# A hybrid SSD, GLA and cross-attention layer on one core: products without priority, a padded row for the convolution, one table at first

## The chip, the core and the metric

The program runs on one core of one Trainium2 chip. Its engines are TensorE (PE in the profile; PEld is its weight load), VectorE (DVE), ScalarE (ACT), GpSimd (POOL) and SyncE (SP), which only issues transfers here. Each engine works its own queue in order and waits on semaphores of the others. The metric is the device time of one execution in microseconds (us).

## The reference

One inference step of one layer, for a prompt of 256 tokens and for 8 samples of 4 tokens each (288 columns together), D_MODEL 2048, everything in float32.

```
xn = rmsnorm(x)
z, xbc, dt, q, k, v, r, g_lr, gate_a, gate_b = split(xn @ w_in)
xbc = silu(causal_conv4(xbc, conv_state))       # 3072 channels, 3 earlier rows per sequence
branch_a = gated_norm(ssd_scan(xbc, dt), z) @ w_ssd_out      # 4 groups of 8 heads
branch_b = gated_norm(gla_scan(q, k, v, g_lr), r) @ w_gla_out   # 4 heads, state 256 x 512 each
h = x + (sigmoid(gate_a)*branch_a + sigmoid(gate_b)*branch_b) @ w_mix_out
h = h + cross_attend(rmsnorm(h), mem_k, mem_v)      # prompt memory is projected here, sample memory is an input
h = h + (silu(g) * a) @ w_down,  a, g = conv3(rmsnorm(h) @ w_up)
```

It returns the normed outputs, the new states of both scans and both convolutions, and the memory keys and values of the prompt.

## The kernel before

Activations lie with channels on the 128 partitions and the 288 tokens along the free axis, columns 0 to 255 for the prompt and 256 to 287 for the samples. Every weight is read once, by SP, in tiles `raw` of 4 x 128 rows by 256 columns (L108). Two halves of such a tile are split into two float32r tiles: `whi` by ACT (L101) and `wlo` by DVE (L103), five buffers each. A projection of 256 output channels (`proj_w`) makes, for one split, 12 products of 288 columns on PE: hi times hi and hi times lo (L133, L134), lo times hi (L137). Its two accumulators lie in two PSUM banks; two pairs of banks alternate. When the last split is through, `cons(j, a)` is called for each of the two output tiles and reads its bank.

The program has these stages: the memory projections with the norms of the memory and of x (from L377, where the statistics use Ln and Exp on ACT at L384, L385, L396, L397, and in `dt_prep`); then eight units, four SSD groups and four GLA heads; the merge; cross-attention; the ConvFFN.

In the eight units, two generators are woven: the projections of unit n + 1, with the output projection of unit n - 1 in their midst, are the main one, and the scan of unit n is the other. `weave` takes `n_bg` steps of the scan per `n_main` steps of the projections; the numbers are N_MAIN and N_BG. A `yield` ends a step. What is written in this order is then ordered per engine by a scheduler that takes the earliest written instruction that it holds ready, with its own estimate of times; an instruction may so pass others. `tc.high_priority(2000)` counts instructions as if they were written 2000 places earlier.

The SSD projections end in `conv_silu` (24 tiles: per group four of x, and for groups 0 and 2 two each of B and C): ACT writes the last tap with the bias from the bank into `out` (L582) and copies what else is wanted out of the bank (L583 to L585); DVE adds the other three taps, for the prompt from the bank (L592), for the samples from a small tile `sp` (L595) whose first three columns POOL has copied from the state (L587); ACT makes the tanh (L597), DVE the product (L598).

In `gla_scan` the samples' states (512 KB each, eight per head) are loaded by POOL's queue into tiles `sin`. Their products with the queries go to one bank `osa` in two groups of four states:

```
        for q in range(2):
            with tc.high_priority(2000):
                for k in (1, 0):
                    for j in (3, 2, 1, 0):
                        ...
                        MM(osa[...], qdm[:, k, b, :], sins[b][:, k, :], start=False, ...)
            yield
            for b in range(4 * q, 4 * q + 4):
                ...  # two products L1101, update of sin on DVE L1102, store by SP L1105, load of state b + 4
```

A tile `sin` of the second four takes the place of an earlier tile, so its load waits for that one's store to land. In `ssd_scan` the states are loaded in the same way (L682), transposed on PE (L833) and updated (L852).

Of the kernel before, what the change touches and what calls it, by code (L numbers as in the profile page):

```python
# [8 lines left out]
F32 = mybir.dt.float32  # L9
F32R = mybir.dt.float32r  # L10
I32 = mybir.dt.int32
ACT = mybir.ActivationFunctionType
ALU = mybir.AluOpType
# [3 lines left out]
P = 128  # L17
D = 2048
KT = D // P
SEQ = 256  # L20
NB = 8
NL = 4
NS = NB * NL
T = SEQ + NS
# [10 lines left out]
STOP = object()  # L35
N_MAIN = [64, 64, 48, 64, 64, 64, 64, 48]
N_BG = [58] * 4 + [42] * 4
# [3 lines left out]
def hybrid_step(ctx: ExitStack, tc: tile.TileContext, I: dict, O: list):  # L41
    nc = tc.nc
    (y_p, y_s, o_pconv, o_pssd, o_pgla, o_pffn, o_pmk, o_pmv, o_sconv, o_sssd, o_sgla, o_sffn) = O
    V, S, G = nc.vector, nc.scalar, nc.gpsimd
    MM, TR = nc.tensor.matmul, nc.tensor.transpose
# [30 lines left out]
    V.memset(epsc[:, 1:2], 4.0 * EPS)  # L76
    S.copy(epsc[:, 2:3], epsc[:, 0:1])
# [6 lines left out]
    vcol = const.tile([P, 116], F32, name="vcol")  # L84
    scw = const.tile([P, 96], F32, name="scw")
# [7 lines left out]
    def vec(name):  # L93
        o, n = vofs[name]
        return vcol[:, o:o + n]
# [133 lines left out]
    dtbd = p1.tile([P, 32 + 8], F32, name="dtbd")[:, 0:32]  # L229
# [5 lines left out]
    scst = p1.tile([P, 24, 24], F32, name="scst")  # L235
# [6 lines left out]
    for z in (cdm, att, ats, atsl.bitcast(F32), qdm, lr3.bitcast(F32), gw3.bitcast(F32), dtbd):  # L242
        G.memset(z, 0.0)
# [8 lines left out]
    with pool("p0") as p0:  # L252
# [170 lines left out]
        def x_prep():  # L423
# [15 lines left out]
            for q in range(2):  # L439
                a = mm_tile()  # L440
                for i in range(3):
                    TR(a[:, i * 96:(i + 1) * 96], srow[:, 3 * q + i, :], ident[0:96, 0:96])
                V.tensor_copy(scst[:, q * 12:(q + 1) * 12, :].rearrange("p t c -> p (t c)"), a[:, 0:288])
                yield
# [118 lines left out]

    def th_tile():
        return pa.tile([P, T], F32, tag="th", bufs=2, name="th")
# [13 lines left out]
    def conv_silu(ct, a, out, cache):  # L579
        cb_o = vofs["ssd_conv_b"][0]  # L580
        sp = pa.tile([P, NB, 8], F32, tag="sp", bufs=3, name="sp")
        S.activation(out, a, ACT.Identity, scale=scw[:, 72 + ct:73 + ct], bias=vcol[:, cb_o + ct:cb_o + ct + 1])  # L582
        S.copy(sp[:, :, 3:7], a[:, SEQ:T].rearrange("p (b l) -> p b l", l=NL))  # L583
        S.copy(cache[:, 0:3], a[:, SEQ - 3:SEQ])
        S.copy(cache[:, 3:27].rearrange("p (b k) -> p b k", k=3),  # L585
               a[:, SEQ:T].rearrange("p (b l) -> p b l", l=NL)[:, :, 1:NL])
        G.tensor_copy(sp[:, :, 0:3], scst[:, ct, :].rearrange("p (b k) -> p b k", k=3))  # L587
        outs = out[:, SEQ:T].rearrange("p (b l) -> p b l", l=NL)
        for k in range(3):
            s = 3 - k  # L590
            w = scw[:, 24 * k + ct:24 * k + ct + 1]
            V.scalar_tensor_tensor(out[:, s:SEQ], a[:, 0:SEQ - s], w, out[:, s:SEQ], ALU.mult, ALU.add)  # L592
        for k in range(3):
            w = scw[:, 24 * k + ct:24 * k + ct + 1]
            V.scalar_tensor_tensor(outs, sp[:, :, k:k + 4], w, outs, ALU.mult, ALU.add)  # L595
        th = th_tile()
        S.activation(th, out, ACT.Tanh)  # L597
        V.scalar_tensor_tensor(out, th, 1.0, out, ALU.add, ALU.mult)  # L598
# [61 lines left out]
    def ssd_scan(g, xsT, sz):  # L660
# [221 lines left out]
        yield  # L882
        yield from finish(sz, acc, vec("ssd_norm")[:, 4 * g:4 * g + 4], True)
# [98 lines left out]
    def gla_scan(h, eb, qe, ke, kd, kde, vT, sr):  # L982
# [104 lines left out]
        for q in range(2):  # L1087
            with tc.high_priority(2000):
                for k in (1, 0):
                    for j in (3, 2, 1, 0):  # L1090
                        b = 4 * q + j
                        MM(osa[NS * j:NS * j + NS, :], qdm[:, k, b, :], sins[b][:, k, :], start=False,
                           stop=(q == 1 and k == 0))
# [573 lines left out]
```

## Time and profile before

| | |
|---|---|
| median of 3 runs | 2626.22 us (2623.78 to 2627.47) |
| the profiled execution | 2624.57 us |
| its span, first to last instruction | 2622.9 us |
| PE busy | 2574.6 us, 98% |
| DVE busy | 1718.3 us, 66% |
| ACT busy | 1375.6 us, 52% |
| POOL busy | 315.1 us, 12% |
| moved from and to memory | 513.55 MB, 196 GB/s |

Busy is the time in which an engine has an instruction in work. Matmuls are pipelined, so a busy PE need not be at its peak. Idle time is put down to the semaphore that ended it. POOL's times are rough.

### The profile page before, as it was taken

The page shows a single profiled execution, that of the slowest core. Times are in us where ns is not written, and L with a number is a line of the kernel's source. Part 1 is how long each engine was busy: PE and PEld are TensorE (multiplying, and loading weights), DVE is VectorE, ACT ScalarE, POOL GpSimd, SP SyncE. Part 2 cuts the span into 40 slices and gives each one's busy share as a digit, 9 for nine tenths or more (in the row PEclk, how much of TensorE's full clock was granted, in tenths as well). Part 3 has the DMA queues.
Part 4 walks back from the last instruction along what each step waited for, and adds up shares of the span by engine and source line. Part 5 has one row for each costly group of instructions (what it writes and reads, how often), then busy time and mean ns, then how long its engine had stood idle before and what let it go on. Part 6 is the DMA issues. An engine that isn't in the chain of part 4 may idle for free. (4 is left out here: it accounts for less than half of the span.)

```text
span 2622.9 us, 50482 instructions
## 1 busy us (share of the span) xinstructions
PE 2574.6 (98%) x19119; PEld 2471.1 (94%) x19119; DVE 1718.3 (66%) x3680; ACT 1375.6 (52%) x2796; POOL 315.1 (12%) x443
## 2 busy tenths in 40 slices
PE   9999999999998999999999999999999999999998
PEld 7889999999997989898999988999999999999998
DVE  5656767686766656667656555567777677675765
ACT  7656456655453545354455544455545454454545
POOL 3002101010000000000000122202202011110200
PEclk9999999999999999999999999999999999999999
DMA  7676666566667565667766778655555555555553
GB/s 259 212 223 190 191 191 214 164 200 190 176 199 244 179 213 182 217 205 228 209 196 224 237 270 273 239 165 161 171 172 166 169 168 169 163 166 172 166 170 127
DMA packets 434768, 513.55 MB, mean 196 GB/s; under 512 B 23208, under 2 KB 384984, under 8 KB 434204
## 3 DMA queue, kind: packets, MB, share of 16 engines
q1 hardware_dynamic: 407532, 420.80, 52.0%
q0 software_dynamic: 26960, 89.52, 10.2%
q8 instruction: 150, 2.46, 0.4%
q14 instruction: 94, 0.77, 0.1%
q10 hardware_dynamic: 32, 0.01, 0.0%
HBM read 464.74 MB, written 45.48 MB: 195 GB/s over the span
## 5 line engine op out<-in xcount | busy, mean ns | idle before, releaser
L103 DVE TENSOR_TENSOR wlo<-raw,whi 128x512 fp32r<-128x512 f32 x1464 | 989.6, 689 | 711.0 <-ACT whi L101 695.6
L101 ACT CAST whi<-raw 128x512 fp32r<-128x512 f32 x1464 | 896.7, 618 | 1024.5 <-PE acc L134 816.0
L133 PE MATMUL acc<-xn,whi 128*128 128x288 f32 (+1 forms) x1936 | 553.9, 301 | 0.0
L134 PE MATMUL acc<-xn,whi 128*128 128x288 f32 (+1 forms) x1936 | 543.1, 296 | 0.0
L137 PE MATMUL acc<-xn,wlo 128*128 128x288 f32 (+1 forms) x1936 | 413.5, 295 | 0.3 <-DVE wlo L103 0.3
L133 PE MATMUL acc<-hf,whi 128*128 128x288 f32 x1408 | 396.5, 296 | 0.0
L134 PE MATMUL acc<-hf,whi 128*128 128x288 f32 x1408 | 393.9, 295 | 0.0
L134 PEld LDWEIGHTS acc<-xn,whi 128*128 128x128 f32 (+1 forms) x1936 | 365.4, 189 | 10.6 <-issue 8.3
L133 PEld LDWEIGHTS acc<-xn,whi 128*128 128x128 f32 (+1 forms) x1936 | 365.0, 189 | 5.8 <-issue 5.0
L137 PEld LDWEIGHTS acc<-xn,wlo 128*128 128x128 f32 (+1 forms) x1936 | 311.6, 188 | 0.9 <-DVE wlo L103 0.6
L137 PE MATMUL acc<-hf,wlo 128*128 128x288 f32 x1408 | 302.7, 297 | 0.0
L134 PEld LDWEIGHTS acc<-hf,whi 128*128 128x128 f32 x1408 | 265.5, 189 | 0.1
L133 PEld LDWEIGHTS acc<-hf,whi 128*128 128x128 f32 x1408 | 265.1, 188 | 0.1
L137 PEld LDWEIGHTS acc<-hf,wlo 128*128 128x128 f32 x1408 | 225.8, 188 | 0.0
L134 PE MATMUL acc<-pr,whi 128*128 128x288 f32 x704 | 196.9, 296 | 0.0
L133 PE MATMUL acc<-pr,whi 128*128 128x288 f32 x704 | 196.0, 294 | 0.0
L133 PE MATMUL acc<-un,whi 128*128 128x288 f32 x512 | 147.5, 304 | 3.8 <-DVE xsT L592 3.8
L137 PE MATMUL acc<-pr,wlo 128*128 128x288 f32 x704 | 148.0, 291 | 0.0
L1499 POOL COPY fsp<-fst 128x16 f32<-128x16 f32 x88 | 106.0, 1229 | 334.8 <-ACT fcg L1505 87.8
L134 PE MATMUL acc<-un,whi 128*128 128x288 f32 x512 | 143.4, 296 | 0.5 <-DVE un L171 0.5
L134 PEld LDWEIGHTS acc<-pr,whi 128*128 128x128 f32 x704 | 132.6, 188 | 0.0
L133 PEld LDWEIGHTS acc<-pr,whi 128*128 128x128 f32 x704 | 132.3, 188 | 0.0
(525 smaller groups left out, 4261.3 us busy)
## 6 DMA issues: line engine op xcount, KB each, us to landing
raw<-in_w_in_dram SPq DMA_DIRECT2D x240, 512.0 KB
raw<-in_w_up_dram SPq DMA_DIRECT2D x176, 512.0 KB
raw<-in_w_down_dram SPq DMA_DIRECT2D x88, 512.0 KB
raw<-in_w_ck_dram SPq DMA_DIRECT2D x32, 512.0 KB
raw<-in_w_cv_dram SPq DMA_DIRECT2D x32, 512.0 KB
raw<-in_w_ssd_out_dram SPq DMA_DIRECT2D x32, 512.0 KB
sin<-in_state_gla_dram POOLq DMA_DIRECT2D x32, 512.0 KB, 5.5
out_dram<-sin SPq DMA_DIRECT2D x32, 512.0 KB
```

What stands on the lines that cost most here:

```text
L101: S.copy(hi, raw)
L103: V.tensor_tensor(lo, raw, hi, ALU.subtract)
L133: MM(a, hi[:, k, cs], xh, start=(k0 + s0 + k == 0), stop=False)
L134: MM(a, hi[:, k, cs], xl, start=False, stop=False)
L137: MM(a, lo[:, k, cs], xh, start=False, stop=(k0 + s0 + k == nk - 1))
L1499: G.tensor_copy(sp[:, :, 0:2], st.rearrange("p (b k) -> p b k", k=2))
```

## The change

Five edits. The products of the sample states are written without `high_priority`. `conv_silu` works on one padded row per tile: eight stretches of 3 old and 4 new columns for the samples, then 3 zeros and the 256 columns of the prompt, 315 in all. ACT copies the bank into it (two copies), then all taps run over 312 columns of it; the tanh overwrites it, and two products write `out`. POOL copies the old rows into it and, from it, what the cache keeps. The padded row and the accumulator take tiles `th`, of which there are now three, shared with the tiles of the gates and scans as before. ACT loads one table that holds Ln and Exp at the start. `ssd_scan` has one more step ahead of the norm's sum, and N_BG grows by one for the SSD groups. `scst` gets room for three zero columns per tile, and is cleared.

```diff
-N_BG = [58] * 4 + [42] * 4
+N_BG = [59] * 4 + [42] * 4
...
+    S.preload_act_table_set(LNEXP)      # LNEXP = "natural_log_exp_and_others"
     S.copy(epsc[:, 2:3], epsc[:, 0:1])
...
-    scst = p1.tile([P, 24, 24], F32, name="scst")
+    scst = p1.tile([P, 24, 3 * NB + 3], F32, name="scst")
...
+    def cv_tile(name):
+        return pa.tile([P, 7 * NB + 3 + SEQ], F32, tag="th", bufs=3, name=name)
+
     def th_tile():
-        return pa.tile([P, T], F32, tag="th", bufs=2, name="th")
+        return cv_tile("th")[:, 0:T]
...
     def conv_silu(ct, a, out, cache):
...
-        S.activation(out, a, ACT.Identity, scale=scw[:, 72 + ct:73 + ct], bias=vcol[:, cb_o + ct:cb_o + ct + 1])
-        S.copy(sp[:, :, 3:7], a[:, SEQ:T].rearrange("p (b l) -> p b l", l=NL))
-        S.copy(cache[:, 0:3], a[:, SEQ - 3:SEQ])
-        S.copy(cache[:, 3:27]..., a[:, SEQ:T]...[:, :, 1:NL])
-        G.tensor_copy(sp[:, :, 0:3], scst[:, ct, :].rearrange("p (b k) -> p b k", k=3))
+        C = 7 * NB
+        cv, acc = cv_tile("cv"), cv_tile("cva")[:, 0:C + SEQ]
+        G.tensor_copy(by7(cv, 0, 3, NB + 1), scst[:, ct, :].rearrange("p (b k) -> p b k", k=3))
+        S.copy(cv[:, C + 3:], a[:, 0:SEQ])
+        S.copy(by7(cv, 3, NL, NB), a[:, SEQ:T].rearrange("p (b l) -> p b l", l=NL))
+        S.activation(acc, cv[:, 3:C + SEQ + 3], ACT.Identity, scale=..., bias=...)
+        G.tensor_copy(cache[:, 0:3], cv[:, C + SEQ:])
+        G.tensor_copy(cache[:, 3:27].rearrange("p (b k) -> p b k", k=3), by7(cv, 4, 3, NB))
         for k in range(3):
-            V.scalar_tensor_tensor(out[:, s:SEQ], a[:, 0:SEQ - s], w, out[:, s:SEQ], ALU.mult, ALU.add)
-        for k in range(3):
-            V.scalar_tensor_tensor(outs, sp[:, :, k:k + 4], w, outs, ALU.mult, ALU.add)
-        th = th_tile()
-        S.activation(th, out, ACT.Tanh)
-        V.scalar_tensor_tensor(out, th, 1.0, out, ALU.add, ALU.mult)
+            V.scalar_tensor_tensor(acc, cv[:, k:k + C + SEQ], scw[...], acc, ALU.mult, ALU.add)
+        th = cv[:, 0:C + SEQ]
+        S.activation(th, acc, ACT.Tanh)
+        V.scalar_tensor_tensor(out[:, 0:SEQ], th[:, C:], 1.0, acc[:, C:], ALU.add, ALU.mult)
+        V.scalar_tensor_tensor(out[:, SEQ:T]..., by7(th, 0, NL, NB), 1.0, by7(acc, 0, NL, NB), ALU.add, ALU.mult)
...
         yield
+        yield
         yield from finish(sz, acc, vec("ssd_norm")[:, 4 * g:4 * g + 4], True)
...
-            with tc.high_priority(2000):
-                for k in (1, 0):
+            for k in (1, 0):
```

In the orders below a line of the changed kernel is 2 to 8 higher than the same line before. First PE, around the second four states of the first GLA head, before: the products `la<-sin` stand in the midst of one split's weight products (`acc<-xn`), behind six of the update products `mm<-vst,kb` (six others stand ahead of these rows).

```order
L137 MATMUL acc<-xn_131,wlo 128x288 x2
L133 MATMUL acc<-xn_131,whi 128x288
L134 MATMUL acc<-xn_131,whi 128x288
L133 MATMUL acc<-xn_131,whi 128x288
L1092 MATMUL la<-sin,qdm 32x512 x8
L134 MATMUL acc<-xn_131,whi 128x288
L137 MATMUL acc<-xn_131,wlo 128x288 x2
L1101 MATMUL mm<-vst,kb 128x512
```

The same engine and place now, 54 rows further on (the products are L1099 here; two update products and 63 weight products have come ahead of them):

```order
L135 MATMUL acc<-xn_134,whi 128x288
L136 MATMUL acc<-xn_134,whi 128x288
L135 MATMUL acc<-xn_134,whi 128x288
L136 MATMUL acc<-xn_134,whi 128x288
L139 MATMUL acc<-xn_134,wlo 128x288 x2
L1099 MATMUL la<-sin,qdm 32x512 x8
L135 MATMUL acc<-xn_134,whi 128x288
```

The second four states now follow all eight update products of the first four; the first four keep their place.

Next ACT, the first two tiles of the convolution, before: `whi` is the weight cast, `acc` the bank that PE has filled, `th` the tanh.

```order
L582 ACTIVATE xsT<-acc,vcol,scw 128x288
L583 COPY sp<-acc 128x8x4
L584 COPY cache<-acc 128x3
L585 COPY cache<-acc 128x24
L101 CAST whi<-raw 128x512
L582 ACTIVATE xsT<-acc,vcol,scw 128x288
L583 COPY sp<-acc 128x8x4
L584 COPY cache<-acc 128x3
L585 COPY cache<-acc 128x24
L101 CAST whi<-raw 128x512
L597 ACTIVATE th<-xsT 128x288
```

And now, where `cv` is the padded row and `cva` the accumulator:

```order
L593 COPY cv<-acc 128x256
L594 COPY cv<-acc 128x8x4
L595 ACTIVATE cva<-cv,vcol,scw 128x312
L593 COPY cv<-acc 128x256
L594 COPY cv<-acc 128x8x4
L103 CAST whi<-raw 128x512 x2
L602 ACT_TABLE_LOAD
L602 ACTIVATE cv<-cva 128x312
L103 CAST whi<-raw 128x512 x2
L595 ACTIVATE cva<-cv,vcol,scw 128x312
L103 CAST whi<-raw 128x512 x2
L602 ACTIVATE cv<-cva 128x312
```

Both banks are read by the first five rows; the second tile's Identity and both tanhs stand between weight casts, and each waits for POOL and DVE.

Last POOL, around the last convolution tiles of the SSD groups and the third scan's states, before: `sp<-scst` is the copy of the old rows, `ab` the decays, `sin` the states of the third and fourth scan.

```order
L668 DMA ab<-acum_d 128x2x256
L587 COPY sp<-scst 128x8x3
L668 DMA ab<-acum_d 128x2x256
L587 COPY sp<-scst 128x8x3
L668 DMA ab<-acum_d 128x2x256
L587 COPY sp<-scst 128x8x3
L682 DMA sin<-in_state_ssd_dram 128x4x128 x16
```

And now:

```order
L592 COPY cv<-scst 128x9x3
L675 DMA ab<-acum_d 128x2x256
L597 COPY cache<-cv 128x3
L598 COPY cache<-cv 128x24
L592 COPY cv<-scst 128x9x3
L597 COPY cache<-cv 128x3
L598 COPY cache<-cv 128x24
L592 COPY cv<-scst 128x9x3
L597 COPY cache<-cv 128x3
L598 COPY cache<-cv 128x24
L689 DMA sin<-in_state_ssd_dram 128x4x128 x16
```

The copy of the old rows needed no result of the convolution's product; the cache copies do, and the state loads now stand behind the last of them.

## Rows read from the trace of the kernel before

**Rows 1.** The page, part 1: busy time, share of the span, instructions.

```profile
PE 2574.6 (98%) x19119; PEld 2471.1 (94%) x19119; DVE 1718.3 (66%) x3680; ACT 1375.6 (52%) x2796; POOL 315.1 (12%) x443
```

**Rows 2.** Waits of PE: who ended them; total us, times, longest us.

```profile
PE la L1092 <- DMA sin<-in_state_gla_dram: 23.6, 4, 7.8
PE acc L133 <- DVE xsT L592: 3.8, 3, 1.6
PE acc L319 <- ACT whi L101: 3.2, 3, 1.7
PE mm L890 <- DVE sqa L881: 1.7, 1, 1.7
```

**Rows 3.** PE's timeline at state products: start us, us, instruction, count, [idle before].

```profile
787.63 1.92 PE L1092 MATMUL la<-sin,qdm 128*32 128x512 f32 x16
...
817.31 3.64 PE L1092 MATMUL la<-sin,qdm 128*32 128x512 f32 x16 [7.76 <-DMA sin<-in_state_gla_dram]
...
946.84 3.64 PE L1092 MATMUL la<-sin,qdm 128*32 128x512 f32 x16 [6.49 <-DMA sin<-in_state_gla_dram]
...
1077.88 2.79 PE L1092 MATMUL la<-sin,qdm 128*32 128x512 f32 x12 [6.20 <-DMA sin<-in_state_gla_dram]
...
1194.39 3.35 PE L1092 MATMUL la<-sin,qdm 128*32 128x512 f32 x16 [3.13 <-DMA sin<-in_state_gla_dram]
```

**Rows 4.** Windows: length, busy (count) of PE, PEld, DVE, ACT, POOL; clock; DMA.

```profile
817.31:822.70 5.39, 5.39 (x23) 2.32 (x24) 0.26 (x1) 1.13 (x2) 0.00 (x0) 0.50 0.00 0
946.84:952.40 5.56, 5.56 (x24) 2.59 (x25) 0.21 (x1) 1.20 (x2) 0.00 (x0) 0.50 0.00 1
1077.88:1082.11 4.23, 4.23 (x19) 1.26 (x20) 0.00 (x0) 0.52 (x2) 0.00 (x0) 0.50 0.04 16
1194.75:1198.16 3.41, 3.41 (x18) 0.93 (x11) 0.00 (x0) 0.38 (x1) 0.00 (x0) 0.50 0.39 138
1700.00:1750.00 50.00, 50.00 (x382) 50.00 (x381) 31.08 (x56) 25.34 (x48) 0.00 (x0) 1.00 0.52 166
```

**Rows 5.** Waits of ACT, the longest.

```profile
ACT whi L101 <- PE acc L134: 816.0, 907, 3.0
```

**Rows 6.** ACT's timeline in the memory projections.

```profile
51.99 1.28 ACT L396 ACT_TABLE_LOAD   x1
...
53.60 1.28 ACT L397 ACT_TABLE_LOAD   x1
```

**Rows 7.** PE's timeline behind those loads, and behind the last convolution pair.

```profile
55.66 0.50 PE L319 MATMUL acc<-whi,mn_hi 128*128 128x512 f32 x1 [1.66 <-ACT whi L101]
...
555.24 0.44 PE L773 MATMUL mm<-m,xdt 128*64 128x128 f32 x4
...
556.70 0.40 PE L133 MATMUL acc<-un,whi 128*128 128x288 f32 x1
```

**Rows 8.** Groups of the convolution: count, busy us, mean ns, idle before.

```profile
L592 DVE SCALAR_TENSOR_TENSOR xsT<-acc,scw,xsT 128x253 f32<-128x253 f32 (+2 forms) x48 | 22.3, 476 | 1.3 <-ACT cache L585 1.3
...
L595 DVE SCALAR_TENSOR_TENSOR xsT<-sp,scw,xsT 128x32 f32<-128x32 f32 x48 | 11.8, 245 | 2.1 <-ACT sp L583 2.1
...
L582 ACT ACTIVATE xsT<-acc,vcol,scw 128x288 f32<-128x288 f32 x16 | 9.7, 604 | 2.1 <-PE acc L137 2.1
...
L587 POOL COPY sp<-scst 128x24 f32<-128x24 f32 x24 | 14.0, 590 | 133.6 <-DVE xsT L595 67.0 <-DVE bc L595 59.3 <-ACT whi L101 7.3
```

**Rows 9.** The line L587: duration ns min/median/max, first and last start.

```profile
L587 POOL COPY sp<-scst x24: 192/216/3053, 207.7 to 543.6; 128x24 f32<-128x24 f32 x24
```

**Rows 10.** POOL's timeline, a long copy and the third scan's state loads.

```profile
221.39 3.05 POOL L587 COPY sp<-scst 128x24 f32<-128x24 f32 x1 [1.84 <-ACT whi L101]
...
543.69 5.92 POOL L682 DMA_DIRECT2D sin<-in_state_ssd_dram  x8
```

**Rows 11.** DVE's timeline beside that long copy.

```profile
223.10 2.06 DVE L103 TENSOR_TENSOR wlo<-raw,whi 128x512 fp32r<-128x512 f32 x3
```

**Rows 12.** The line L682, the SSD state loads: issue to landing.

```profile
DMA to landing us min/median/max: 3.1/5.5/7.8
```

More of the change, by code (lines that the diff above doesn't have):

```diff
@@ L35 @@
 STOP = object()
+LNEXP = "natural_log_exp_and_others"
 N_MAIN = [64, 64, 48, 64, 64, 64, 64, 48]
-N_BG = [58] * 4 + [42] * 4
+N_BG = [59] * 4 + [42] * 4
 @with_exitstack
@@ L228, in hybrid_step @@
     gw3 = p1.tile([P, 256], F32R, name="gw3")
-    dtbd = p1.tile([P, 32 + 8], F32, name="dtbd")[:, 0:32]
+    dtbd = p1.tile([P, 32], F32, name="dtbd")
     acs = p1.tile([P, 8], F32, name="acs")
@@ L241, in hybrid_step @@
     qdm = p1.tile([P, 2, NB, NS], F32, name="qdm")
-    for z in (cdm, att, ats, atsl.bitcast(F32), qdm, lr3.bitcast(F32), gw3.bitcast(F32), dtbd):
+    for z in (cdm, att, ats, atsl.bitcast(F32), qdm, lr3.bitcast(F32), gw3.bitcast(F32), dtbd, scst):
         G.memset(z, 0.0)
@@ L442, in x_prep @@
                     TR(a[:, i * 96:(i + 1) * 96], srow[:, 3 * q + i, :], ident[0:96, 0:96])
-                V.tensor_copy(scst[:, q * 12:(q + 1) * 12, :].rearrange("p t c -> p (t c)"), a[:, 0:288])
+                V.tensor_copy(scst[:, q * 12:(q + 1) * 12, 0:3 * NB], a[:, 0:288].rearrange("p (t c) -> p t c", c=3 * NB))
                 yield
@@ L580, in conv_silu @@
         cb_o = vofs["ssd_conv_b"][0]
-        sp = pa.tile([P, NB, 8], F32, tag="sp", bufs=3, name="sp")
-        S.activation(out, a, ACT.Identity, scale=scw[:, 72 + ct:73 + ct], bias=vcol[:, cb_o + ct:cb_o + ct + 1])
-        S.copy(sp[:, :, 3:7], a[:, SEQ:T].rearrange("p (b l) -> p b l", l=NL))
-        S.copy(cache[:, 0:3], a[:, SEQ - 3:SEQ])
-        S.copy(cache[:, 3:27].rearrange("p (b k) -> p b k", k=3),
-               a[:, SEQ:T].rearrange("p (b l) -> p b l", l=NL)[:, :, 1:NL])
-        G.tensor_copy(sp[:, :, 0:3], scst[:, ct, :].rearrange("p (b k) -> p b k", k=3))
@@ L588, in conv_silu @@
-        outs = out[:, SEQ:T].rearrange("p (b l) -> p b l", l=NL)
-        for k in range(3):
-            s = 3 - k
-            w = scw[:, 24 * k + ct:24 * k + ct + 1]
-            V.scalar_tensor_tensor(out[:, s:SEQ], a[:, 0:SEQ - s], w, out[:, s:SEQ], ALU.mult, ALU.add)
-        for k in range(3):
-            w = scw[:, 24 * k + ct:24 * k + ct + 1]
-            V.scalar_tensor_tensor(outs, sp[:, :, k:k + 4], w, outs, ALU.mult, ALU.add)
-        th = th_tile()
-        S.activation(th, out, ACT.Tanh)
@@ L598, in conv_silu, with by7 @@
-        V.scalar_tensor_tensor(out, th, 1.0, out, ALU.add, ALU.mult)
+        C = 7 * NB
+        cv, acc = cv_tile("cv"), cv_tile("cva")[:, 0:C + SEQ]
+        def by7(t, o, n, m):
+            return t[:, o:o + 7 * (m - 1) + n] if m == 1 else bass.AP(t.tensor, t.offset + o, [list(t.ap[0]), [7, m], [1, n]])
+        G.tensor_copy(by7(cv, 0, 3, NB + 1), scst[:, ct, :].rearrange("p (b k) -> p b k", k=3))
+        S.copy(cv[:, C + 3:], a[:, 0:SEQ])
+        S.copy(by7(cv, 3, NL, NB), a[:, SEQ:T].rearrange("p (b l) -> p b l", l=NL))
@@ new lines, in conv_silu @@
+        S.activation(acc, cv[:, 3:C + SEQ + 3], ACT.Identity, scale=scw[:, 72 + ct:73 + ct],
+                     bias=vcol[:, cb_o + ct:cb_o + ct + 1])
+        G.tensor_copy(cache[:, 0:3], cv[:, C + SEQ:])
+        G.tensor_copy(cache[:, 3:27].rearrange("p (b k) -> p b k", k=3), by7(cv, 4, 3, NB))
+        for k in range(3):
+            V.scalar_tensor_tensor(acc, cv[:, k:k + C + SEQ], scw[:, 24 * k + ct:24 * k + ct + 1], acc, ALU.mult, ALU.add)
+        th = cv[:, 0:C + SEQ]
+        S.activation(th, acc, ACT.Tanh)
@@ L600, in silu2 @@
+        V.scalar_tensor_tensor(out[:, 0:SEQ], th[:, C:], 1.0, acc[:, C:], ALU.add, ALU.mult)
+        V.scalar_tensor_tensor(out[:, SEQ:T].rearrange("p (b l) -> p b l", l=NL), by7(th, 0, NL, NB), 1.0,
+                               by7(acc, 0, NL, NB), ALU.add, ALU.mult)
     def silu2(a, out):
@@ L1087, in gla_scan @@
         for q in range(2):
-            with tc.high_priority(2000):
-                for k in (1, 0):
[L1090 to L1093, printed above, removed]
+            for k in (1, 0):
+                for j in (3, 2, 1, 0):
+                    b = 4 * q + j
+                    MM(osa[NS * j:NS * j + NS, :], qdm[:, k, b, :], sins[b][:, k, :], start=False,
+                       stop=(q == 1 and k == 0))
             yield
```

## The prediction, as it was recorded

> **What bounds the kernel now.** I read the page first: TensorE (PE) is busy in 2574.6 us of a span of 2622.9 [rows 1]. The change removes no matrix product, so PE's busy time can fall only where PE works slowly; the rest to be had is its idle time, 48.3 us. The waits of PE, longest first, say who ends that idle time [rows 2]: 23.6 us in four waits for GLA states to land (products of L1092), 3.8 us in three for the convolution to give a PSUM bank back (L592), 3.2 us in three for a weight split at the start (L319), 1.7 us in one for a sum of squares (L890). Then I looked at the four long waits in PE's timeline [rows 3]: 7.76, 6.49, 6.20 and 3.13 us, all at the second four states of a GLA head. What the waits view does not show stands beside them: a group of 16 records takes 1.92 us at 787.63, and 3.64 right behind a wait. The windows after the four waits [rows 4] give the reason: the granted clock is 0.50 (the level of 1.2 GHz; PE idled before it fell), against 1.00 (2.4 GHz) elsewhere. So each of these waits is paid twice, once idle and once at half speed.
>
> The other engines have room. ScalarE (ACT) waits 816 us in total for PE to release a weight buffer [rows 5]: it runs ahead of PE as far as the five buffers let it.
>
> **Part 1, the products without priority.** The same 64 products are issued; only their place on PE changes. The first four states of a head keep their place; the second four move behind the last two of the eight update products (PE's order, above). Ahead of them come 63, 77, 75 and 40 weight products in the four heads, and those two. A weight product costs 50.00/382 = 0.131 us in a full stretch [rows 4], so PE comes 8.3, 10.1, 9.8 and 5.2 us later to the second group, without the update products. The states landed 7.76, 6.49, 6.20 and 3.13 us after PE stood there. What gates a landing (the update of an earlier state, its store on SP's queue, the reload on POOL's) keeps its order in this stage. So all four waits end before PE arrives, the first by the narrowest margin, 0.5 us plus the two update products. Gain 23.6 us. The scaling copy of the finished sum on ACT comes later too, but it already waits there today, and ACT stands about five splits ahead of PE then.
>
> The half clock goes with the waits: the windows are 5.39, 5.56, 4.23 and 3.41 us long [rows 4], and at full clock the same work needs half of that. Gain 18.59/2 = 9.3 us.
>
> **Part 2, one table at first.** Six table loads go from ACT in the stage of the memory projections. One pair stands just ahead of a late split: loads at 51.99 and 53.60, of 1.28 us each [rows 6]; the cast behind them ends PE's idle 1.66 us at 55.66 [rows 7]. Without 2 × 1.28 us it comes before PE does. Gain 1.7 us. The other 1.5 us of the waits at L319 end on other casts, away from the removed loads; I count nothing, at most those 1.5.
>
> **Part 3, the convolution.** Today one tile holds its bank through ACT's L582 (604 ns) and three L592 on VectorE (DVE), 476 ns each, with three short L595 between them [rows 8]. Now ACT copies the bank out in two instructions and it is free; both tiles' banks are empty after some 2 us even at 0.6 us for a copy. The next pair in these banks comes at the earliest 24 products of 0.131 us after it. Gain: the 3.8 us of L592. ACT has one more long instruction per tile, about 0.6 us × 24 = 14 us over some 350 us, covered by its waiting for PE [rows 5]. DVE's three products of 312 columns cost about what 3 × (476 + 245) ns cost. The extra step before the sum of squares moves its product behind a split: gain 1.7 us (L890).
>
> What it adds is waits on POOL. POOL now makes three small copies per tile: the old rows into the padded row, and two into the cache. ACT's Identity waits for the first, its Tanh for the other two, since Tanh overwrites the padded row; behind the Tanh in ACT's queue stand weight casts, and PE waits for those. One such copy takes 216 ns at the median, 3053 at most [rows 9] and 590 on the mean [rows 8]; the longest, at 221.39 [rows 10], ran beside DVE's back-to-back splits [rows 11]. From below: six copies a pair at 0.2 us are hidden behind ACT's lead of four splits, 48 × 0.131 = 6.3 us of PE's work, so nothing. From above: six at 3.05 us are 18.3 us, 12 us past the lead. At the mean a pair's six are 3.5 us, under 6.3, so I stay near the lower end and take 2 us in all.
>
> The Trainium skill speaks against this part: GPSIMD Engine Reference, § 1. Specifications, says that GpSimd shares its SBUF interfaces with VectorE and is held up by VectorE instructions with two SBUF inputs. The old L592 read one input from PSUM; the new products read both from SBUF. The trace agrees as far as it goes: the 3.05 us copy lay beside L103, whose two inputs are in SBUF [rows 11]. By that rule long copies get commoner; the last rival prices it.
>
> The cache copies stand ahead of DMAs on POOL. In the third SSD scan the state loads were issued at 543.69, ahead of the convolution of the last pair [rows 10]; now they come behind that pair's last cache copies (POOL's order, above). When does PE want the first state? Between the pair's last product and the first transposes stand, in the new order, 28 short products and transposes and 36 weight products. By the timeline the short ones ahead of the first weight product take 1.5 us (from 555.24 to 556.70 [rows 7]), four transposes about 0.5, 36 × 0.131 = 4.7: PE is there after 6.7 us. The load is issued after the bank copies, one cast, one Identity and two POOL copies, 2 to 3 us after the last product, and lands 3.1 to 7.8 us later, median 5.5 [rows 12]. Wait: 2.5 + 5.5 − 6.7 = 1.3 us; at least none; at most, with two POOL copies of 3.05 and the longest landing, 2 + 6.1 + 7.8 − 6.7 = 9.2. Every wait over 3 us above was followed by half speed, so I take 2.5 us for it.
>
> **The sum.** 23.6 + 9.3 + 1.7 + 3.8 + 1.7 = 40.1; less 2 and 2.5 is 35.6 us. The profiled execution took 2624.57 (its span and 1.7 around it): 2589.0. The median of the runs is 1.65 above the profiled one, so 2590.6; I say 2590, and 2582 to 2598 for this case by itself.
>
> **Rivals.**
> - The state loads of the third SSD scan become the new wait. For it: the loads stand behind six waiting POOL instructions, and DMA is busy in that stage. Against: DMA is less loaded by 8 transfers just before. At 9.2 us and the 2.3 us that the half clock costs on the mean (9.3/4), against the 2.5 counted: 2590 + 9.0 = 2599.
> - The change does not do what it says: the products arrive later and still wait, since the loads move too. For it: the first head has a margin of about 1 us, and loads of states differ by 4.7 us from landing to landing [rows 12]. Against: the order of what gates the loads is unchanged. With half of 23.6 + 9.3 kept: 2590 + 16.5 = 2606.
> - No new wait at all: 2590 − 4.5 = 2586, and down to 2582 with the small waits that I left.
> - Slower: POOL's copies hold ACT in every pair. The place is the Tanh of L602 and the Identity of L595; it decides from 6.3 us of held ACT per pair on. At 12 us per pair (the bounds are 1.2 and 18.3), 12 pairs × 5.7 us = 68 us: 2590 + 68 = 2658. It is slower than today from 9.3 us per pair. Against it: while ACT is held it feeds DVE no casts, DVE falls idle, and the copy goes through.
>
> **How the numbers follow.** Chances: the forecast 0.60; the state loads 0.13; products still waiting 0.11; no new wait 0.11; POOL slower 0.05. The range must hold 0.8: forecast, no new wait, the state loads and most of the third case lie in 2580 to 2608. What a measurement of this kernel can tell from no change is 0.2%, 5.3 us. Faster than 2621 are all cases but the last and a worse form of the second: 0.93; within 0.2%: 0.03; slower: 0.04.
>
> **What would show it.** Right: no wait of PE on GLA states, no window at 0.50 between 812 and 1199; no PE wait on the convolution; the first ACT table load after the first one at the first Tanh; PE's busy time lower by about 9 us. Part 3 as costed: copies at L592, L597 and L598 on POOL mostly near 0.2 us, and waits for them on ACT that no PE wait follows. Wrong: a PE wait for SSD states in the third scan over 5 us, or PE waits on weight splits between 217 and 565 that add up to more than the 3.8 us won there.

## The result and the profile after

The kernel takes 2579.45 us (median of 4 runs, 2579.14 to 2580.91) against 2625.0 (2622.37 to 2627.47): a ratio of 0.9828, with a 95% interval of 0.9811 to 0.9845, or 45.6 us less. I forecast 2590 and said 2580 to 2608, so the direction was right and the time lies 0.55 us below the range. The profiled execution took 2579.59 us, with a span of 2577.9; that is 45.0 us less than the span before.

The page of the kernel after, part 1 (before: [rows 1]): busy time, share of the span, instructions.

```profile
PE 2560.0 (99%) x19119; PEld 2464.7 (96%) x19119; DVE 1715.9 (67%) x3632; ACT 1376.3 (53%) x2767; POOL 321.2 (12%) x492
```

The products are the same 19119. PE is busy 14.6 us less than before and idle 30.4 us less, 17.9 in place of 48.3. So a third of the gain doesn't appear as a wait in the profile before. The longest waits of PE after (before: [rows 2]), total us, times, longest us:

```profile
PE acc L321 <- ACT whi L103: 1.9, 2, 1.0
PE mm L898 <- DVE sqa L1006: 1.4, 1, 1.4
PE mm L352 <- DVE epsc L76: 1.1, 1, 1.1
PE mm L288 <- DMA mt<-in_mem_prompt_dram: 0.9, 1, 0.9
```

No wait on a GLA or SSD state is left, none on the convolution, and what remains are small single waits. PE's timeline of the first GLA head's state products (before: [rows 3]), and windows that hold the second four of each head, which now start at 807.80, 930.82, 1052.60 and 1158.77 us, and all four heads (before: [rows 4]):

```profile
777.27 1.92 PE L1099 MATMUL la<-sin,qdm 128*32 128x512 f32 x16
807.80 1.92 PE L1099 MATMUL la<-sin,qdm 128*32 128x512 f32 x16
```

```profile
806.00:816.00 10.00, 10.00 (x78) 8.32 (x77) 4.83 (x9) 4.30 (x8) 0.00 (x0) 1.00 0.66 210
929.00:939.00 10.00, 10.00 (x77) 8.32 (x76) 4.89 (x9) 4.39 (x8) 0.00 (x0) 1.00 0.56 159
1051.00:1061.00 10.00, 10.00 (x77) 8.32 (x77) 5.11 (x9) 4.40 (x8) 0.00 (x0) 1.00 0.64 192
1156.00:1166.00 10.00, 10.00 (x77) 8.32 (x77) 7.01 (x14) 3.20 (x6) 0.00 (x0) 1.00 0.71 234
776.00:1200.00 424.00, 421.99 (x3143) 398.73 (x3142) 284.97 (x564) 215.55 (x381) 26.55 (x41) 1.00 0.71 226
```

Both groups of the first head now take 1.92 us, the time of the first group before, and the granted clock (the number after the five engines) is 1.00 throughout.

The convolution's products on VectorE (before: [rows 8]), the first table load behind the one at the start (before: [rows 6]), and ScalarE's longest wait (before: [rows 5]):

```profile
L600 DVE SCALAR_TENSOR_TENSOR cva<-cv,scw,cva 128x312 f32<-128x312 f32 x72 | 38.9, 541 | 11.6 <-ACT cva L595 10.3
```

```profile
219.02 1.28 ACT L602 ACT_TABLE_LOAD   x1 [0.82 <-DVE cva L600]
```

```profile
ACT whi L103 <- PE acc L136: 810.7, 900, 3.9
```

Three products of 541 ns do the work of three pairs of 476 and 245; no table is loaded any more between the first one and the first Tanh; and ScalarE still runs ahead of PE.

To see where the time came from I cut PE's work at fixed matmuls, which stand at nearly the same work in every kernel (of a few the neighbour has changed places). This table is worked out from PE's records: us from the start of one matmul to the start of the other, and in brackets the idle time that the records' waits show in it (37.2 of the 48.3 us before).

| PE's matmuls (us in the kernel before) | before | part 1 alone | part 3 alone | after |
|---|---|---|---|---|
| 0 to 600 (1 to 133), memory projections | 131.5 (3.8) | 132.5 (5.7) | 133.9 (5.3) | 130.0 (2.8) |
| 600 to 1100 (to 226) | 93.4 (0) | 93.4 (0) | 93.4 (0) | 93.4 (0) |
| 1100 to 4900 (to 720), SSD scans, convolution | 493.8 (7.3) | 494.7 (7.5) | 483.7 (0) | 483.7 (0) |
| 4900 to 5400 (to 787) | 66.8 (0) | 66.8 (0) | 68.0 (0.6) | 68.0 (0.6) |
| 5400 to 8300 (to 1211), GLA scans | 423.9 (23.7) | 390.3 (0.5) | 423.5 (24.4) | 391.2 (1.5) |
| from 8300 on | 1402.2 (2.4) | 1400.1 (1.7) | 1400.5 (1.7) | 1400.1 (1.7) |

The two middle columns are the first two experiments below. Part 1 shortens the GLA row and part 3 the row of the SSD scans. The last row is some 2 us shorter in both, though neither edit touches it.

One profile stands behind each column, and a row can differ without an edit in its stage. In the kernels below that keep the code of before in a stage, the SSD row took 493.8 to 498.6 us (six kernels, the one before being the shortest), the GLA row 419.7 to 424.1 (five kernels) and the last row 1400.1 to 1402.2. So a difference of 2 us in one of these rows shows nothing by itself, and the 10 us of part 3 are counted from the low end.

### The profile page after: what moved, and what is told of

It reads as the page before. It is cut to its first block, busy times and chain, and to the rows that moved or that the text cites. A ratio compares the mean times of both kernels' runs of the same rounds, so it can differ in the third digit from the quotient of the medians.

```text
span 2577.9 us, 50452 instructions
## 1 busy us (share of the span) xinstructions
PE 2560.0 (99%) x19119; PEld 2464.7 (96%) x19119; DVE 1715.9 (67%) x3632; ACT 1376.3 (53%) x2767; POOL 321.2 (12%) x492
## 3 DMA queue, kind: packets, MB, share of 16 engines
q0 software_dynamic: 26960, 89.52, 10.4%
```

## The experiments

Times are medians; each ratio is to runs of the kernel before on the same chip (2624.6 to 2626.4 us), with its 95% interval.

**Part 1 alone.**

```
-            with tc.high_priority(2000):
-                for k in (1, 0): ...
+            for k in (1, 0): ...
```

> The kernel before with part 1 alone (the second four state products of a GLA head without priority). Theory A (each of the four waits is paid twice, once idle and once at half clock): 23.6 us of waits and 9.3 us of half clock go, 33 us, so 2592 us against 2625; no PE wait on GLA states, no stretch at a granted clock of 0.50 between 812 and 1199 us, PE's busy time 9 to 10 us lower. Theory B (the half clock stands behind something else, a neighbour of the waits): 23.6 us go alone, 2601 us, and PE's busy time stays within 2 us. Theory C (part 1 gave more than I counted, all of the unexplained 10 us are here): 2582 us.

Measured: 2590.8 us, ratio 0.9866 (0.9849 to 0.9883), 33.8 us less by the medians. Theory A holds: the GLA row falls by 33.6 us, of which 23.2 are idle time and 10.4 busy time.

**Part 3 alone.** The diff is that of the change without its first and its table parts.

> The kernel before with part 3 alone (padded row, copies out of the bank, cache copies on GpSimd, one more step before the sum of squares). Theory A (the bank waits of 3.8 us, the 1.7 us at the sum of squares and some small waits of the same stage go, and the copies on GpSimd cost nothing): 9 to 11 us faster, 2614 to 2616 us against 2625, and PE's busy time between 200 and 720 us is 3 us lower. Theory B (the recorded sum: 3.8 + 1.7 less 4.5 for the copies and the later state loads): 1 us faster, 2624 us. PE keeps its four waits on GLA states (23.6 us) under both.

Measured: 2613.3 us, ratio 0.9947 (0.9932 to 0.9962), 11.2 us less. The recorded sum, theory B, falls. In the SSD row all 7.3 us of idle time go, and 2.8 us of busy time with them.

**Part 2 alone.**

```
+    S.preload_act_table_set(LNEXP)
     S.copy(epsc[:, 2:3], epsc[:, 0:1])
```

> The kernel before with part 2 alone (one table loaded at the start). Both theories agree on the place: PE's wait at 55.66 us (1.66 us) is gone or under 0.3 us. Theory A: 1.7 us faster, which is inside what the measurement can tell (2623 against 2625). Theory B (the other casts of that stage were also late because of the removed loads): 3 us, 2622 us, and all three waits on the split of L319 are gone. Theory C: the next wait in line takes its place, and nothing is won.

Measured: 2623.5 us, ratio 0.9991 (0.9980 to 1.0001): not told from no change. The wait at 55.66 is gone, as both theories said, and the wait before it is longer than it was before (0.63 us at 40.06). PE's timeline of this run:

```profile
41.86 0.50 PE L321 MATMUL acc<-whi,mn_hi 128*128 128x512 f32 x1 [2.52 <-ACT whi L103]
```

But this wait differs between runs whose code there is the same in what matters (0.92 in part 1 alone, 2.91 in part 3 alone), so one profile doesn't show that it took the place of the other. Whether theory A or C holds stays open. The three parts alone, 33.8 + 11.2 + 1.1 = 46.1, add up to the whole, 45.6, within the noise.

**Filling the wait, first try.** 100 products with zero weights, ahead of the second four states, priority kept:

```
 with tc.high_priority(2000):
+    for _ in range((33, 28, 26, 13)[h] if q else 0):
+        MM(osa, zst, vst, start=False, stop=False)
     for k in (1, 0):
```

> The kernel before, with the priority kept, and 33, 28, 26 and 13 products with a zero weight tile put on PE ahead of the second four states of the four GLA heads (they add zero to the sum). At about 0.23 us each they take 7.6, 6.4, 6.0 and 3.0 us, about as long as PE waited there (7.76, 6.49, 6.20, 3.13). So the states still land as late as before, and PE is no longer idle until then. Theory A (the clock falls because PE idles, and each wait is paid a second time at half clock): the waits are under 0.5 us each, no stretch at 0.50 follows, and the kernel is 9 to 10 us faster, 2615.5 against 2625. Theory B (the slow stretch behind the waits has to do with the products or the states, not with PE's idling): the stretches at 0.50 stay and the time stays at 2625.

Measured: 2644.8 us, ratio 1.0072 (1.0056 to 1.0089). It tells neither theory from the other, since the products didn't stand directly ahead of the second four states. PE's timeline:

```profile
791.45 7.84 PE L1091 MATMUL la<-vst,zst 128*128 128x512 f32 x33
...
826.06 3.64 PE L1095 MATMUL la<-sin,qdm 128*32 128x512 f32 x16 [7.00 <-DMA sin<-in_state_gla_dram]
```

Nothing held them back, so the priority brought them right behind the first four states. There they put off the update products, and with these the stores and the reloads: the states landed 8.75 us later (817.31 in [rows 3]) than before, and the wait stayed. This shows in passing that PE's own update products gate the landing.

**Filling the wait in place.** The zero tile is now made from the sixth update's result, so that the products can't start earlier:

```
+                    if b == 2 and k == 1:
+                        V.tensor_scalar(zst, sin[:, 1, 0:P], 0.0, None, ALU.mult)
```

> The filling run again, with the products on zero weights held back until the sixth update product's result is written (the zero tile is made from it), so that they stand directly ahead of the second four states: 33, 28, 26 and 13 products, 7.6, 6.4, 6.0 and 3.0 us. In the first filling run they stood 26 us earlier, behind the first four states, put off the update products whose results gate the loads, and the waits stayed. Theory A (each wait is paid a second time because PE idled): PE's waits on GLA states fall from 23.6 to under 3 us, no stretch at 0.50 between 812 and 1199 us, and the kernel is 8 to 10 us faster than before, 2615 to 2617. Theory B (the slow stretch comes with the products or the states): stretches at 0.50 remain and the time stays within 3 us of before.

Measured: 2619.5 us, ratio 0.998 (0.997 to 0.9989), 5.7 us less; I expected 8 to 10. PE's timeline of the first head, and the windows behind it:

```profile
814.46 7.73 PE L1091 MATMUL la<-vst,zst 128*128 128x512 f32 x33
822.44 1.92 PE L1095 MATMUL la<-sin,qdm 128*32 128x512 f32 x16 [0.25 <-DMA sin<-in_state_gla_dram]
```

```profile
820.00:1060.00 240.00, 239.66 (x1755) 225.27 (x1754) 145.09 (x287) 123.47 (x222) 12.99 (x20) 1.00 0.63 196
1194.00:1215.00 21.00, 20.65 (x141) 18.19 (x142) 13.79 (x26) 6.60 (x11) 0.00 (x0) 0.92 0.53 162
```

The states land as late as ever, PE has 100 products more to do, and the kernel is faster. In the three heads where the filling covers the wait the state products take 1.92 us and the clock stays at 1.00 (in the third head over 1060 to 1100 us). In the fourth a wait of 2.40 us is left, and the clock falls (0.92 over that window). In the GLA row idle time falls by 20.9 us and busy time rises by 15.6; the filling is 100 × 0.234 = 23.4 us (33 in 7.73), so 7.8 us of slow work are gone, the fourth head's missing. So the half clock comes from PE's idling, not from the products or the states. Less came than I expected since the filling took 2.5 us more than the idle time that it replaced (23.4 less 20.9): the row gains 7.8 − 2.5 = 5.3 us.

**The bank copied out, nothing else of part 3.** The copy needs a third tile `th`.

```
-        return pa.tile([P, T], F32, tag="th", bufs=2, name="th")
+        return pa.tile([P, T], F32, tag="th", bufs=3, name="th")
...
+        ac = th_tile()
+        S.copy(ac, a)
+        a = ac
         S.activation(out, a, ACT.Identity, ...)
```

> The kernel before with one thing of part 3: ScalarE copies the bank of each tile into SBUF at once, and everything else of the convolution (six products on VectorE, cache copies on ScalarE, one step before the sum of squares) works as before, but from that copy. In PE's stage of the SSD scans (226 to 720 us) the kernel before took 493.8 us and the kernel with part 3 alone 483.7. Theory A (the bank held through VectorE's products is what cost there): the waits on the convolution's products (3.8 us) go, 4 to 6 us faster, 2619 to 2621. Theory B (the shorter chain of one row on VectorE is needed too): under 2 us faster, since the new copy of 0.6 us a tile lengthens the chain as much as the early release shortens PE's wait. Theory C (VectorE reads faster from SBUF, and nearly the whole 10 us come from the copy): 9 us or more, 2616 or less.

Measured: 2622.6 us, ratio 0.9988 (0.9978 to 0.9997), 2.5 us less: between A and B, and the interval reaches into both. PE's waits on the convolution's products are gone, but new ones of 1.1 us (on the low half of a weight split) and 0.7 us (on the cache) stand in their place, and the SSD row is 491.9 us against 493.8. An early release of the bank alone is a small part of the 10 us. What the single padded row gives without the rest was not run by itself.

**One step before the sum of squares.**

```
-        yield
         yield
         yield from finish(sz, acc, ...)
```

> The kernel after without the extra step before the sum of squares (and with the old count of 58). Theory A (the step was worth the 1.7 us of the wait at L890): PE's wait on the sum of squares is back, 1.7 to 3.2 us, and the kernel is 2 us slower than the kernel after, 2581.5, ratio 0.9835. Theory B (with the convolution's shorter chain the sum of squares comes in time without the step): no wait, no change, ratio 0.9828.

Measured: 2586.4 us, ratio 0.9846 (0.9833 to 0.9860), some 5 us more than the kernel after by the ratios (0.0018 × 2625). PE's timeline, and the window that begins with that product:

```profile
512.38 0.75 PE L897 MATMUL mm<-sqa,ones 128*128 128x288 f32 x2 [2.28 <-DVE sqa L888]
```

```profile
512.38:518.00 5.62, 5.62 (x29) 5.51 (x30) 2.38 (x5) 4.21 (x7) 0.54 (x1) 0.70 0.48 132
```

Here too the wait of 2.28 us is paid twice: the SSD row is 489.0 us against 483.7, 2.5 idle and 2.8 slow. In the stretch behind it (4900 to 5400) the step costs 1.2 us, 68.0 against 66.8. So it nets 4.1 us in these two rows. I had put 1.7 on it. The last row took 1402.3 us here, 2.2 more than in the kernel after, without an edit there.

**Cache copies back on ScalarE.**

```
-        G.tensor_copy(cache[:, 0:3], ...)      (and [:, 3:27])
+        S.copy(cache[:, 0:3], ...)
```

> The kernel after with the two cache copies of each tile back on ScalarE (from the padded row). Theory A (the copies on GpSimd cost nothing, and the third SSD scan's state loads land in time behind them): no change against the kernel after, ratio to before 0.982 to 0.984, 2578 to 2582 us; no PE wait on weight splits or state loads appears or goes. Theory B (the terms of 2 and 2.5 us that I took off are there, hidden in small waits): up to 4.5 us faster than the kernel after, 2575 us, ratio 0.981. Theory C (ScalarE needs the room that the copies on GpSimd gave it): slower than the kernel after by 2 us or more.

Measured: 2579.4 us, ratio 0.9830 (0.9813 to 0.9848), and the SSD row is 483.7 us to the tenth. The cache copies on GpSimd cost nothing, and the later state loads (issued at 550.49, here at 549.35) nothing either. Their lines in the kernel after (duration ns min/median/max, first and last start; before: [rows 9]):

```profile
L597 POOL COPY cache<-cv x24: 187/282/387, 216.2 to 549.9; 128x3 f32<-128x3 f32 x24
...
L598 POOL COPY cache<-cv x24: 199/222/695, 216.3 to 550.2; 128x24 f32<-128x24 f32 x24
```

**Cache copies 16 times over.**

```
+        for _ in range(16):
             G.tensor_copy(cache[:, 0:3], ...)   (and [:, 3:27])
```

> The kernel after with each pair of cache copies on GpSimd issued 16 times over (same data to the same place). Two copies take 0.26 us from start to start in the kernel after, so a tile gets 15 x 0.26 = 3.9 us more and a pair of tiles 7.8. The state loads of the third SSD scan come 7.8 us later and PE waits there some 6 us under every theory. Theory A (my slower rival as worked out: ScalarE is held until the last copy, its lead over PE is 6.3 us of weight products per pair, and nothing else runs beside): 2.3 us a pair over the lead, 12 pairs, 28 us slower than the kernel after, about 2610, and waits of PE on weight splits between 217 and 565 us. Theory B (the copies run beside VectorE's three products of 0.53 us a tile, which Tanh waits for anyway, so only 4.6 us of a pair hold ScalarE, inside its lead): only the late state loads count, 6 to 8 us slower than the kernel after, about 2587. Theory C (nothing is hidden): 12 x 7.8 = 94 us slower, 2673.

Measured: 2655.5 us, ratio 1.0122 (1.0103 to 1.0141), 76 us over the kernel after: more than A, less than C. The wait at the state loads is 13.0 us, where I expected some 6 under every theory. The waits show a place that none of the theories named:

```profile
PE mm L575 <- POOL cache L599: 42.0, 4, 15.1
PE mm L841 <- DMA sin<-in_state_ssd_dram: 13.0, 1, 13.0
```

ScalarE was held 73.5 us in 16 Tanh, as my slower rival had it, but PE waited for weight splits hardly at all. It waited where it reads the cache itself, at the transpose behind every four tiles. After the first of these waits PE ran at half clock:

```profile
249.00:252.00 3.00, 3.00 (x13) 3.00 (x14) 0.00 (x0) 0.45 (x2) 0.00 (x0) 0.50 0.01 2
```

**State loads of the third SSD scan held back.** Sixteen clears of a tile on GpSimd ahead of them. The first kernel also added a tile of 16 bytes:

```
+    sink = p1.tile([P, 4], F32, name="sink")        (first run only)
+        if g == 2:
+            G.tensor_copy(qf[:, 0:27], last[-1][:, 0:27])
+            for _ in range(16):
+                G.memset(qf, 0.0)
+            G.tensor_copy(sink, qf[:, 0:4])          (first run only)
         load_state(0)
```

> The kernel after with 16 clears of a 512-column tile on GpSimd (about 0.47 us each, 7.5 us) behind the last cache copies and ahead of the state loads of the third SSD scan. Theory A (after has a margin there: the first load landed 1.66 us before PE stood at the first transposes): PE waits 7.5 less 1.7 = 5.8 us for the states, a stretch at a granted clock of 0.50 follows and costs about 2 us, 8 us slower than the kernel after, 2587, ratio 0.986. Theory B (my recorded term: at the median landing the loads are already 1.3 us late): a wait of about 8.8 us and 11 us slower, 2590. Theory C (the transposes can wait without cost, since other work fills in): no wait and the time of the kernel after.

Measured: 2594.4 us, ratio 0.9881 (0.9864 to 0.9898), 15 us over the kernel after. Only 5.5 us of that lie near the loads (3.4 idle, 2.0 slow); the rest is a slightly slower PE from 47 us on.

> The run with the late state loads again, without the 16-byte tile that it added in SBUF. In that run PE waited 2.5 and 0.9 us for the states of the third SSD scan and worked about 2 us at half clock behind, 5.5 us, but some 9 us more came from a pace of PE 1 to 2% slower between 47 and 700 us, far from the loads. Theory A (the pace hangs on where the tiles lie in SBUF; the 16 bytes moved them): the slow pace is gone and only the waits are left, 5 to 6 us slower than the kernel after, 2585, ratio 0.985. Theory B (the pace has another reason): 2594 again.

Measured, without the 16 bytes: 2582.9 us, ratio 0.9835 (0.9821 to 0.9848), 3.4 us over the kernel after (I expected 5 to 6). The slow pace is gone, as theory A said: matmuls 600 to 1100 take 93.4 us again, 95.2 with the 16 bytes. GpSimd and PE in this run:

```profile
560.27 5.91 POOL L692 DMA_DIRECT2D sin<-in_state_ssd_dram  x8
```

```profile
563.52 0.66 PE L848 MATMUL mm<-ident,sin 128*128 128x128 f32 x4 [1.94 <-DMA sin<-in_state_ssd_dram]
```

And the same two places in the kernel after:

```profile
550.49 5.92 POOL L689 DMA_DIRECT2D sin<-in_state_ssd_dram  x8
```

```profile
555.36 0.60 PE L840 MATMUL mm<-ident,sin 128*128 128x128 f32 x4
```

The loads were issued 9.8 us later, and the order on PE moved the first transposes 6.2 us back (PE came at 561.58). With its first landing 3.2 us after issue, 553.7, the kernel after has 1.66 us to spare: 9.8 − 6.2 − 1.7 = 1.9, the wait seen. So the margin of the first run's theory A is confirmed, though its wait of 5.8 us was too long, since I had not thought of the order.

**Moving the tiles by 16, 64 and 256 bytes.**

```
 after, 16 bytes:    dtbd = p1.tile([P, 32 + 4], ...)[:, 0:32]
 after, 64 bytes:    dtbd = p1.tile([P, 32 + 16], ...)[:, 0:32]
 before, 256 bytes:  dtbd = p1.tile([P, 32 + 8 + 64], ...)[:, 0:32]
```

> The kernel after with one tile 16 bytes longer (dtbd, 36 columns of which 32 are used), so that all tiles behind it lie 16 bytes further in SBUF, and nothing else. Theory A (PE's pace hangs on where the tiles lie): 7 to 9 us slower than the kernel after, 2587 to 2589, ratio 0.986, with PE's records in the memory projections 1 to 2% longer. Theory B (it doesn't): the time of the kernel after, 2579.5, ratio 0.983.

> The kernel after with the tile dtbd 64 bytes longer in place of 16. Theory A (what matters is where a tile starts within a piece of 64 bytes): the time of the kernel after, ratio 0.983, records of L322 at 389 ns. Theory B (any move away from this layout costs): 7 to 10 us slower, ratio 0.986, records of L322 at 395 ns.

> The kernel before with dtbd 256 bytes longer, so that the tiles behind it lie 256 bytes further in SBUF, as the longer scst makes it in the kernel after; nothing else. Theory A (the layout took no part in the gain): the time of before, ratio 0.999 to 1.001, and the stage of the memory projections (PE's matmuls 600 to 1100) takes 93.4 us as in before and after. Theory B (part of the gain is the layout): 3 us or more faster, ratio 0.9988 or less, with PE's busy time lower in the stage of the SSD scans.

Measured: 2589.6 us, ratio 0.9861 (0.9848 to 0.9875); 2591.2, ratio 0.9866 (0.9853 to 0.9879); 2625.0, ratio 0.9995 (0.9985 to 1.0005). One line of PE in the memory projections, in the kernel after, then 16 bytes on, then 64 bytes on:

```profile
L322 PE MATMUL acc<-whi,mn_lo x256: 387/389/402, 8.3 to 202.9; 128*128 128x512 f32 x128
```

```profile
L322 PE MATMUL acc<-whi,mn_lo x256: 392/395/403, 8.3 to 207.5; 128*128 128x512 f32 x128
```

```profile
L322 PE MATMUL acc<-whi,mn_lo x256: 388/398/628, 9.1 to 210.7; 128*128 128x512 f32 x128
```

In the kernel after, 16 or 64 bytes cost 9 to 10 us by the ratios, with hardly more waits of PE (7.5 and 7.9 us in all, against 7.4). Some 3 us of this lie in the last row (1403.0 and 1403.3 us, against 1400.1), which is about as long in kernels whose tiles didn't move (with one step, and in the next experiment), so 6 to 7 us go with the move. It shows best in matmuls 600 to 1100, which have no waits: 93.4 us in every kernel here but the three whose tiles moved by 16 or 64 bytes, 95.2, 95.2 and 95.5. In the kernel before, 256 bytes cost nothing. So my guess of pieces of 64 bytes is wrong; why 16 and 64 bytes cost time stays open.

The change moves the tiles behind scst by 256 bytes (288 more for scst, 32 fewer for dtbd), so that shift is no part of its gain. It also moves the five tiles made between the two by 32 bytes, and in the pool of the scans `th` grows and `sp` goes; these shifts were not run by themselves.

**The steps placed better.** The extra step in the first three SSD scans only, and one in each GLA scan:

```
-        yield                          (SSD scan)
+        if g < 3:
+            yield
+        yield                          (GLA scan, ahead of finish)
```

> The kernel after with the extra step before the sum of squares in the first three SSD scans alone, and an extra step before the sum of squares in the four GLA scans. Theory A (the step costs 1.2 us in the last SSD scan, where PE came to wait for the sum of squares, and would win 1.3 us at 844.57 in the first GLA scan): 2 to 2.5 us faster than the kernel after, 2577, ratio 0.982, and no PE wait on a sum of squares over 0.5 us. Theory B (a moved step opens a wait of the same size elsewhere): the time of the kernel after within 1 us.

Measured: 2580.9 us, ratio 0.9828 (0.9814 to 0.9842): the time of the kernel after. The two waits are gone (66.6 in place of 68.0 us, no idle time in the GLA row), but in this profile the stretch from matmul 8300 on, which the edit doesn't touch, takes 1403.1 us in place of 1400.1. That stretch took 1400.1 to 1401.7 us in most kernels and 1402.2 to 1403.3 in before, with one step, with 16 and 64 bytes, and here. In the last four the excess stands at the same products to within 0.1 us, though from matmul 8435 on PE's order is that of the kernel after, so it is not an accident of one execution. I found no cause. It is of the size of the gain that I looked for, so the verdict on the two theories stays open; no new wait of that size opened elsewhere.

## Why the prediction was right in direction and too small

By its own terms, in us of the span; the middle column is the row of the table of stretches to which each belongs.

| Term of the prediction | forecast | measured |
|---|---|---|
| GLA waits 23.6 and half clock 9.3 | 32.9 | 32.7 (5400 to 8300) |
| table at first | 1.7 | 1.5 (0 to 600; alone, it can't be told from nothing) |
| convolution 3.8, step 1.7, less 2 (copies) and 2.5 (state loads) | 1.0 | 10.1 (1100 to 4900) |
| not forecast | 0 | −1.2 (4900 to 5400), 2.1 (from 8300; there without an edit too) |
| sum | 35.6 | 45.2, of a span of 45.0 |

**Part 1** came as worked out, wait for wait and with the slow stretch behind each. Part 1 alone gave 33.8 us. That the row agrees to 0.2 us is in part luck: counted from the other kernels with the GLA code of before it would be 28.5 to 32.9. That idle time is the cause of the half clock, which I had only read from neighbouring rows, is now shown by the run that fills the waits in place.

**The step that failed is the one about part 3.** It took off two costs that did not come, and put small waits and slow work of the same stage at nothing. Of the 9.1 us missing there:
- 4.5 us are the two costs that I took off, and neither came. For the copies on GpSimd I chose 2 us between 0 and 12; they stayed at 0.2 to 0.7 us, and putting the two cache copies on ScalarE changed nothing. For the state loads I chose 2.5 us from a median landing of 5.5. The issue came 2.0 us after the last product and PE 6.8 us after it, as I had worked out (2 to 3, and 6.7), but the first landing took 3.2 us, near the least in [rows 12]. The transposes need the first load of eight, and that one isn't a median load: the first of eight landed after 3.0 to 3.2 us in all three batches of the kernel after, and after 3.1 to 4.6 in those of before. At 4.6 PE would still have found it there.
- 1.4 us are a wait on wst (L845) behind the last pair. It stands in the trace before, but I didn't count it. It went by the order on PE: in the kernel after 16 more products stand ahead of that place (it is matmul 3745 in place of 3729), and so they do in the run that copies the bank out and nothing else, where wst comes 0.5 us later than before (570.08 against 569.61) and PE reads it without a wait at 571.47.
- 0.4 us are one wait at the start of the stage, and 2.8 us are busy time in which PE went slower. Part of such time can be half clock behind small waits, as the kernel with one step shows; but in before itself the windows around its waits in that stage (431 to 445, 514 to 530, 561.8 to 580 us) are at 1.00. Cut into stretches of 50 matmuls, 1.6 of the 2.8 us lie in the five that hold the stage's six waits, some 0.3 us a wait; the rest isn't traced to rows and stays open.

I also mis-sized the step before the sum of squares. Where the wait is 1.73 us, as before, the clock stays; at 2.28 and 3.18 us (the latter in the run of the table alone) it fell to 0.70 and 0.50 in the windows behind. The length of the wait alone doesn't decide this: behind the wait of 2.52 us at 41.86 in the run of the table alone the clock stayed at 1.00, and behind 1.94 us at 563.52 in the second run with late loads it was 0.69 over 5.5 us. In the kernels that keep the code of before in that stage the wait took 1.7 to 3.2 us, so the profile before showed the cheap form of it.

**The rivals.** "No new wait at all", 2586 down to 2582, was the case that came, and it went 2.5 us further. The state loads and the waiting products did not come. The slower rival's mechanism is real, at 16 times the copies, but PE would pay at the cache's transpose, not at the weight splits.

**The rule on GpSimd and VectorE.** The Trainium skill (GPSIMD Engine Reference, § 1. Specifications) says that GpSimd shares its SBUF interfaces with VectorE and names contention with VectorE instructions that have two SBUF inputs. The trace of the kernel after agrees, with a small price. The copies of the old rows, and the longest of them beside two splits on VectorE:

```profile
L592 POOL COPY cv<-scst x24: 207/212/616, 206.1 to 548.6; 128x27 f32<-128x27 f32 x24
```

```profile
221.47 0.62 POOL L592 COPY cv<-scst 128x27 f32<-128x27 f32 x1 [3.97 <-DVE xsT L604]
```

```profile
221.32 1.30 DVE L105 TENSOR_TENSOR wlo<-raw,whi 128x512 fp32r<-128x512 f32 x2
```

Six of the 24 copies began while such an instruction ran and had more than 0.2 us of it ahead; they took 0.37 to 0.62 us and ended some 0.07 us behind it. The other 18 took 0.21 to 0.22 us. So long copies did not get commoner, as I feared: the mean of all 72 copies is 0.27 us in place of 0.59, the longest 0.7, and copies held over several splits, as the 3.05 us of before [rows 10], did not come back.

## What to carry to other kernels

A wait of the bound engine should be priced with what runs slowly behind it, and the small waits of one stage belong together: here they were six of 0.4 to 1.7 us, and part 3 removed them all. A cost that is bounded between nothing and something large, on an engine off the path, is better left in the range than taken off the sum. Where the first of several loads is what is waited for, the landing of the first of a batch is the number to use, not the median of all.

## What the runs showed that I had not expected

- PE's pace changed with where tiles lie in SBUF. With most tiles moved by 16 or 64 bytes the kernel after took 9 to 10 us more of 2580, 6 to 7 of them beside the open swing of the last row (records of 395 and 398 ns in place of 389), and no wait shows it; 256 bytes cost the kernel before nothing. An experiment that adds a small tile can measure that too.
- Adding 23.4 us of products to the bound engine made the kernel 5.7 us faster, since they stood in idle time and kept the granted clock at 1.00.
